# Gating and rounding of the output weights' pieces: kept in their traced place, one microsecond of plan time later

## The chip, the cores and the metric

The kernel runs on one core of a Trainium2 chip. The metric is the device time of one execution in microseconds (us). A core has a matrix engine (TensorE; PE in the rows, its weight loads PEld), VectorE (DVE), ScalarE (ACT), GpSimd (POOL) and SyncE (SP), whose queue issues nearly all DMAs here. Each of these takes its instructions strictly in the order in which they were laid down, so an instruction that waits holds up all that stands behind it on the same engine.

## The reference, cut to what matters

One layer of a diffusion trunk over 2048 latent tokens of width 1024, with 256 context tokens ahead of it. The part that the change touches is the output projection of the first half of the layer, whose columns are scaled by a gate:

```python
o, _, _ = token_mixers(h @ w_in[l], lb_f, lb_b, first, hf_c, hb_c, *mix_args)
x = x + g1 * (o @ w_out[l])
```

`g1` is one row of 1024 numbers that comes from the conditioning vector. `token_mixers` is a gated linear recurrence (four heads, two directions) and a spatial gating unit, both fed by the one big projection `h @ w_in`.

## The kernel before, in words

The tokens are taken in two halves of 1024. For each half the kernel runs a row of "banks": one bank is 128 output columns of `h @ w_in` for 512 tokens, eight k-steps of three matmuls each (each operand is split into a rounded high part and a rest, and high x high, low x high, high x low are summed: `xh`, `xl` for the tokens, `whi`, `wlo` for the weights). A weight block of 128 columns serves two banks. It is loaded as `raw` (L213, 512 KB), cast to `whi` on ACT (L131) and subtracted to `wlo` on DVE (L132). Between the k-steps the kernel calls two pumps. One, `hg_q`, feeds the work of the recurrence heads (matmuls on `Q` and `K` into `sc`, then on ACT, DVE and POOL the level updates: L500, L507, L578, L580, L802). The other, `bg_q`, feeds background work: the gate rows (`ada_block`), then the output weights (`w_out_ops`), the convolution taps and the down weights. A generator in a pump runs up to its next `yield w` and is resumed when the planned TensorE time has gone on by `w` us.

`w_out_ops` goes over 16 pieces of 128 x 512. A piece takes one of the three `raw` buffers, which it shares with the weight blocks of L213. One half of the buffer gets the weights (L945), the other the gate row spread over 128 partitions (L946). Later DVE multiplies them (L949), ACT rounds the product into `wo_hi` (L131, in a single buffer that is free again when the store of the piece before has landed), DVE subtracts for the low part (L132), and SP stores both to `wo_d` in DRAM (L951, L952), from where the output projection reads them much later (from 903 us on).

What is traced is then laid down by a scheduler, which may let an instruction pass others of its engine where it expects that they wait. `pin` (`keep_in_program_order`) forbids that for one instruction: it keeps its place in the traced order. In `split` the argument `keep` is applied to the ACT copy alone.

```python
def split(hi, lo, raw, eng=None, keep=lambda i: i):
    keep(S.copy(hi, raw))
    (eng or G).tensor_sub(lo, raw, hi.bitcast(F32))
```

When the last bank of half 0 is traced, the tokens of half 1 are loaded into `xh` and `xl` (L1069, L1070: 16 loads of 512 KB, each as soon as TensorE has used the old rows of its k-steps), and the banks of half 1 follow.

Of the kernel before, what the change touches and what calls it, by code (L numbers as in the profile page):

```python
# [10 lines left out]
F32R = mybir.dt.float32r  # L11
# [72 lines left out]
def tile_trunk(ctx, tc, x, c, cx, c_ctx, w_ada, b_ada, norm_mix, norm_ffn, w_in, hg_norm, sgu_g, sgu_b,  # L84
               w_sp, b_sp, w_out, w_up, conv_w, conv_b, w_down, norm_final, masks, out):
    nc = tc.nc
    V, S, G, T = nc.vector, nc.scalar, nc.gpsimd, Tensor(nc.tensor)
    ld = nc.sync.dma_start
    st = nc.sync.dma_start
    pin = tc.keep_in_program_order  # L90
# [38 lines left out]
# [4 lines that stand above are left out]
# [56 lines left out]
    with es1:  # L189
# [16 lines left out]
        def raw_tile():  # L206
            return p1.tile([P, D], F32, tag="raw", name="raw", bufs=3)
# [730 lines left out]
        def w_out_ops():  # L938

            for k in range(NK):  # L940
                for n in range(2):
                    cl = slice(n * 512, n * 512 + 512)
                    raw = raw_tile()
                    w, g = raw[:, :512], raw[:, 512:]
                    ld(w, w_out[k * P:(k + 1) * P, cl])  # L945
                    ld(g, g_d[0:1, cl].broadcast_to([P, 512]))  # L946
                    yield 5.0
                    hi = pm.tile([P, 512], F32, tag="acc", name="wo_hi")
                    V.tensor_mul(w, w, g)  # L949
                    split(hi.bitcast(F32R), g.bitcast(F32R), w, V)  # L950
                    st(wo_d[:, k, 0, cl], hi)  # L951
                    st(wo_d[:, k, 1, cl], g)  # L952
                    yield 2.5

        def w_down_ops():

# [19 lines left out]
        def head(hh, h):  # L976
# [18 lines left out]
            def pre_g():  # L995
                if prev[0] >= 0:
                    need(hg_q, (prev[0], prev[1], "keys"))
                else:
                    need(bg_q, "x1")
                    for e in range(8):  # L1000
                        bg_q.add(ada_block(e))
                    bg_q.add(w_out_ops())
                    bg_q.add(conv_taps())
                    bg_q.add(w_down_ops())
                t["F"] = pk.tile([P, 2, TH], F32, tag="F", name="F", align_bytes=AL)
                t["K"] = pk.tile([P, 2, TH], F32, tag="K", name="K", bufs=2, align_bytes=AL)
# [508 lines left out]
    for n, (u, i) in enumerate(prods):  # L1515
# [7 lines left out]
        hi, lo = u.A[i]  # L1523
# [37 lines left out]
    V = Kept(nc.vector, pin)  # L1561
# [243 lines left out]
```

## Time and profile before

| | us |
|---|---|
| three runs | 2458.63, 2462.23, 2462.24 |
| their median | 2462.23 |
| the profiled execution, own time | 2459.64 |
| its span in the trace | 2457.9 |
| TensorE busy | 2417.9 |
| VectorE busy | 1790.2 |
| ScalarE busy | 970.5 |
| GpSimd busy | 882.5 |

The span is the time from the first to the last instruction that the trace records. 1.7 us of the execution's own time lie outside it. Matmuls are pipelined, so that their recorded durations overlap (0.39 us each, 0.227 us from start to start).

### The profile page before, as it was taken

How to read it: one execution, taken by the hardware profiler on the slowest of the kernel's cores; microseconds unless marked ns; L12 is line 12 of the kernel's file. 1: busy time of each engine (PE TensorE's matmuls, PEld its weight loads, DVE VectorE, ACT ScalarE, POOL GpSimd, SP SyncE). 2: the span in 40 equal slices, each digit the busy share in tenths (PEclk: the TensorE clock that was granted, in tenths of full speed). 3: DMA queues.
4: the chain of work that ended last, by engine and by line, in shares of the span. 5: the costliest groups of instructions: out<-in, count | busy, mean ns of one | idle time of the engine just before them, and what ended most of it. 6: DMA issues, size and time to landing. Idle time of an engine off the chain costs nothing.

```text
span 2457.9 us, 32777 instructions
## 1 busy us (share of the span) xinstructions
PE 2417.9 (98%) x11859; PEld 2008.3 (82%) x11859; DVE 1790.2 (73%) x2445; ACT 970.5 (39%) x1614; POOL 882.5 (36%) x795
## 2 busy tenths in 40 slices
PE   7999999999999999999999999999999999999998
PEld 4888888888888888788788888888888888888887
DVE  5867785845766766465698878759999992776875
ACT  4554344434344442354443333333333342332343
POOL 1232110110121122100688787787777870000002
PEclk9999999999999999999999999999999999999999
DMA  8365446664354333768922222462222239844745
GB/s 308 109 208 164 146 129 202 198 214 146 103 180 155 99 103 104 260 205 269 300 90 85 91 80 90 163 250 93 84 89 94 87 102 348 312 127 147 227 150 197
DMA packets 307854, 400.12 MB, mean 163 GB/s; under 512 B 33113, under 2 KB 216161, under 8 KB 304621
## 3 DMA queue, kind: packets, MB, share of 16 engines
q1 hardware_dynamic: 304404, 397.28, 48.7%
q8 instruction: 94, 1.54, 0.3%
q10 hardware_dynamic: 3289, 0.76, 0.1%
q14 instruction: 67, 0.55, 0.1%
HBM read 288.85 MB, written 109.13 MB: 162 GB/s over the span
## 4 chain that ended last, share of the span: by engine, by line
PE 45%; DVE 7%; issue 3%; POOL 2%; ACT 2%; DMA 1%; SPq 0%; POOLq 0%; ACTq 0%; DVEq 0%
PE up L65 24%; PE dn L65 20%; DVE dn L1372 3%; DVE edges L1377 1%; DVE gp L1453 1%; ACT dn L1369 1%; POOL Al L132 1%; PE up L69 0%; PE pj L65 0%; POOL ra L1664 0%; DMA raw<-oT 0%; DMA xn<-cv 0%; POOL rr L1665 0%; DMA raw<-in_w_up_dram 0%; DVE keep L1447 0%
## 5 line engine op out<-in xcount | busy, mean ns | idle before, releaser
L1372 DVE SCALAR_TENSOR_TENSOR dn<-gp,taps,dn 128x1024 f32<-128x1024 f32 x352 | 448.2, 1279 | 21.3 <-ACT dn L1369 18.1
L65 PE MATMUL up<-yf,Ah 128*128 128x512 f32 x1232 | 393.6, 389 | 0.0
L65 PE MATMUL dn<-thl,mhl 128*128 128x512 f32 x1680 | 381.5, 389 | 1.2 <-ACT thl L131 1.2
L132 POOL TENSOR_TENSOR Al<-raw,Ah 128x512 fp32r<-128x512 f32 x264 | 343.3, 1309 | 87.8 <-ACT Ah L131 79.7
L65 PEld LDWEIGHTS dn<-thl,mhl 128*128 128x128 f32 x1680 | 315.1, 188 | 67.6 <-ACT thl L131 2.0
L65 PE MATMUL pj<-xh,whi 128*128 128x512 f32 x896 | 363.7, 406 | 0.0
L65 PE MATMUL pj<-xh,wlo 128*128 128x512 f32 x896 | 350.5, 391 | 3.0 <-DVE wlo L132 3.0
L65 PE MATMUL pj<-xl,whi 128*128 128x512 f32 x896 | 351.2, 392 | 1.0 <-POOL xl L132 1.0
L65 PE MATMUL up<-xah,Al 128*128 128x512 f32 x704 | 275.4, 391 | 2.9 <-POOL Al L132 2.8
L65 PE MATMUL up<-xah,Ah 128*128 128x512 f32 x704 | 274.5, 390 | 0.6 <-ACT Ah L131 0.6
L131 ACT CAST Ah<-raw 128x512 fp32r<-128x512 f32 x264 | 160.6, 618 | 278.5 <-PE up L65 212.3
L65 PEld LDWEIGHTS up<-yf,Ah 128*128 128x128 f32 x1232 | 231.2, 188 | 47.9
L65 PE MATMUL up<-xal,Ah 128*128 128x512 f32 x528 | 205.4, 389 | 0.0
L65 PE MATMUL up<-yf,Al 128*128 128x512 f32 x528 | 205.2, 389 | 0.0
L65 PEld LDWEIGHTS pj<-xh,wlo 128*128 128x128 f32 x896 | 168.3, 188 | 39.4 <-DVE wlo L132 3.7
L65 PEld LDWEIGHTS pj<-xh,whi 128*128 128x128 f32 x896 | 168.7, 188 | 33.2 <-issue 3.5
L65 PEld LDWEIGHTS pj<-xl,whi 128*128 128x128 f32 x896 | 168.9, 189 | 31.6 <-POOL xl L132 1.9
L65 PE MATMUL dn<-wo,o 128*128 128x512 f32 x768 | 182.9, 394 | 1.7 <-ACT o L131 1.1
L65 PEld LDWEIGHTS dn<-wo,o 128*128 128x128 f32 x768 | 141.9, 188 | 31.4 <-ACT o L131 1.6
L578 POOL TENSOR_TENSOR K<-K,tot 128x512 f32<-128x512 f32 x40 | 57.4, 1434 | 306.4 <-ACT K L580 222.4
L65 PEld LDWEIGHTS up<-xah,Al 128*128 128x128 f32 x704 | 132.1, 188 | 35.5 <-POOL Al L132 8.3
L132 DVE TENSOR_TENSOR wlo<-raw,whi 128x1024 fp32r<-128x1024 f32 x68 | 83.8, 1232 | 99.7 <-ACT whi L131 93.4
(315 smaller groups left out, 4021.6 us busy)
## 6 DMA issues: line engine op xcount, KB each, us to landing
raw<-in_w_up_dram SPq DMA_DIRECT2D x88, 512.0 KB, 4.6
mr<-m SPq DMA_DIRECT2D x85, 512.0 KB, 5.3
raw<-in_w_in_dram SPq DMA_DIRECT2D x68, 512.0 KB, 4.4
sT<-wd SPq DMA_DIRECT2D x88, 256.0 KB, 4.0
raw<-in_w_ada_dram SPq DMA_DIRECT2D x32, 512.0 KB, 4.0
yf<-yd SPq DMA_DIRECT2D x14, 1024.0 KB
m<-cv SPq DMA_DIRECT2D x22, 544.0 KB, 2.7
raw<-in_w_down_dram SPq DMA_DIRECT2D x22, 512.0 KB, 4.5
```

The lines of the kernel that those rows point to most:

```text
L65: return self.engine.matmul(out, lhsT, rhs, **kw)
L131: keep(S.copy(hi, raw))
L132: (eng or G).tensor_sub(lo, raw, hi.bitcast(F32))
L578: e.tensor_mul(view(K2, a * (2 * B + W), [[4 * B, n], [W + B - 2 * a * W, 2], [1, B]]), view(K, a * 2 * B, src), t)
L1369: S.activation(cr, gt[:, 0:RH, 0:GW], AF.Identity, bias=cvb[:, f:f + 1], scale=taps[:, f:f + 1])
L1372: V.scalar_tensor_tensor(out=cr, in0=gt[:, t // 3:t // 3 + RH, t % 3:t % 3 + GW], scalar=taps[:, t * NF + f:t * NF + f + 1], in1=cr, op0=A ...
L1377: V.scalar_tensor_tensor(out=e[:, 0, :], in0=gt[:, 1, t % 3:t % 3 + GW], scalar=taps[:, t * NF + f:t * NF + f + 1], in1=e[:, 0, :], op0=AL ...
L1453: V.tensor_add(g_rows(hh, f + c, n2), quad(p, kind), quad(add, kind))
```

## The change

The wait between the request for a piece and its gating grows from 5 to 6 us of planned TensorE time, and the wait to the next piece shrinks by as much. The product (L949) and the rounding copy (L131 into `wo_hi`) are pinned. The subtraction and the stores aren't.

```diff
                     ld(w, w_out[k * P:(k + 1) * P, cl])
                     ld(g, g_d[0:1, cl].broadcast_to([P, 512]))
-                    yield 5.0
+                    yield 6.0
                     hi = pm.tile([P, 512], F32, tag="acc", name="wo_hi")
-                    V.tensor_mul(w, w, g)
-                    split(hi.bitcast(F32R), g.bitcast(F32R), w, V)
+                    pin(V.tensor_mul(w, w, g))
+                    split(hi.bitcast(F32R), g.bitcast(F32R), w, V, pin)
                     st(wo_d[:, k, 0, cl], hi)
                     st(wo_d[:, k, 1, cl], g)
-                    yield 2.5
+                    yield 1.5
```

No instruction is added or taken away; their order changes. Three places follow.

VectorE at the end of head 2's gate banks of half 0. `wlo_3621` is the low part of the next weight block; `raw_3695` and `raw_3574` are pieces of the output weights. Before:

```order
L949 TENSOR_TENSOR raw_3634<-raw_3634 128x512
L132 TENSOR_TENSOR raw_3634<-raw_3634,wo_hi_3677 128x512
L949 TENSOR_TENSOR raw_3695<-raw_3695 128x512
L132 TENSOR_TENSOR wlo_3621<-raw_3618,whi_3620 128x1024
L779 TENSOR_TENSOR Q_3668<-qs_3174,F_3442 128x1024
```

And of the change:

```order
L949 TENSOR_TENSOR raw_3574<-raw_3574 128x512
L132 TENSOR_TENSOR raw_3574<-raw_3574,wo_hi_3607 128x512
L132 TENSOR_TENSOR wlo_3621<-raw_3618,whi_3620 128x1024
L779 TENSOR_TENSOR Q_3668<-qs_3174,F_3442 128x1024
L949 TENSOR_TENSOR raw_3631<-raw_3631 128x512
```

The fifth piece's product stood ahead of `wlo_3621`; now the third piece's work stands there, and the fourth product comes behind it.

SyncE where the tokens of half 1 are loaded. Before, the two weight blocks `raw_4529` and `raw_4617` are requested ahead of all 16 token loads, and no piece is among them:

```order
L213 DMA raw_4529<-in_w_in_dram 128x8x128
L674 DMA oT0_77<-nt_4257 128x512
L213 DMA raw_4617<-in_w_in_dram 128x8x128
L484 DMA tr_4650<-in_conv_w_dram 99x128
L1070 DMA xl_357<-xl_d_80 128x2x512
L1069 DMA xh_358<-xh_d_79 128x2x512 x2
L1070 DMA xl_357<-xl_d_80 128x2x512
```

The change, from the 14th piece's stores on; ten token loads stand behind the 15th's:

```order
L951 DMA wo_d_81<-wo_hi_4437 128x512
L952 DMA wo_d_81<-raw_4403 128x512
L1070 DMA xl_357<-xl_d_80 128x2x512
L1069 DMA xh_358<-xh_d_79 128x2x512
L945 DMA raw_4508<-in_w_out_dram 128x512
L946 DMA raw_4508<-g_d_76 128x512
L1070 DMA xl_357<-xl_d_80 128x2x512
L951 DMA wo_d_81<-wo_hi_4491 128x512
L952 DMA wo_d_81<-raw_4452 128x512
L1069 DMA xh_358<-xh_d_79 128x2x512
```

Its end, where `raw_4529` and `raw_4617` are requested behind the last token load:

```order
L1069 DMA xh_358<-xh_d_79 128x2x512
L1070 DMA xl_357<-xl_d_80 128x2x512
L213 DMA raw_4529<-in_w_in_dram 128x8x128
L951 DMA wo_d_81<-wo_hi_4572 128x512
L952 DMA wo_d_81<-raw_4508 128x512
L213 DMA raw_4617<-in_w_in_dram 128x8x128
```

The pieces and the two weight blocks have changed places around the token loads.

ScalarE at the start of half 1. `sig_4565` and `sig_4614` belong to the first two banks of half 1 (`pj_4535` and `pj_4574`, which the change calls `pj_4568`); `whi_4531` is the weight block of the third. Before:

```order
L131 CAST whi_4531<-raw_4529 128x1024
L553 ACTIVATE F_4362<-pj_4475 128x512
L558 ACTIVATE K_4363<-pj_4475 128x256x2
L972 ACTIVATE sig_4565<-pj_4535 128x512
L787 COPY sc_4584<-sc_4585 128x512
L787 COPY sc_4584<-sc_4591 128x512
L131 CAST whi_4619<-raw_4617 128x1024
L972 ACTIVATE sig_4614<-pj_4574 128x512
```

And of the change:

```order
L787 COPY sc_4584<-sc_4585 128x512
L972 ACTIVATE sig_4565<-pj_4535 128x512
L787 COPY sc_4584<-sc_4591 128x512
L131 CAST wo_hi_4572<-raw_4508 128x512
L972 ACTIVATE sig_4614<-pj_4568 128x512
L131 CAST whi_4531<-raw_4529 128x1024
L131 CAST whi_4619<-raw_4617 128x1024
```

The cast of the third bank's weights moved from ahead of the first bank's sigmoid to behind the second's. On VectorE its subtraction (`wlo_4532`) stands likewise behind the product with that sigmoid (`sgt`, L973).

## Rows read from the trace of the kernel before

**Rows 1.** The page's busy times: engine, busy us, share, instructions.

```profile
PE 2417.9 (98%) x11859; PEld 2008.3 (82%) x11859; DVE 1790.2 (73%) x2445; ACT 970.5 (39%) x1614; POOL 882.5 (36%) x795
```

**Rows 2.** Windows: stretch, length, busy us by engine, TensorE clock, DMA share, GB/s.

```profile
395.00:410.00 15.00, 15.00 (x70) 12.32 (x68) 2.63 (x4) 6.46 (x10) 0.00 (x0) 1.00 0.57 196
410.00:425.00 15.00, 12.89 (x65) 10.76 (x65) 11.30 (x13) 6.29 (x10) 0.00 (x0) 1.00 0.53 175
440.00:530.00 90.00, 89.99 (x499) 77.48 (x499) 50.60 (x86) 36.47 (x55) 10.60 (x10) 1.00 0.76 255
```

**Rows 3.** Waits of TensorE, 365 to 600 us: in total, times, longest.

```profile
PE pj L65 <- DVE wlo L132: 2.1, 1, 2.1
PE sc L65 <- ACT K L580: 1.2, 2, 0.8
```

**Rows 4.** Timeline of TensorE: start, length, what, idle before it.

```profile
409.84 0.39 PE L65 MATMUL pj<-xl,whi 128*128 128x512 f32 x1
412.34 0.50 PE L65 MATMUL pj<-xh,wlo 128*128 128x512 f32 x1 [2.11 <-DVE wlo L132]
```

**Rows 5.** Timeline of VectorE there.

```profile
410.46 0.69 DVE L949 TENSOR_TENSOR raw<-raw 128x512 f32<-128x512 f32 x1 [10.54 <-DMA raw<-g_d]
411.07 1.22 DVE L132 TENSOR_TENSOR wlo<-raw,whi 128x1024 fp32r<-128x1024 f32 x1
```

**Rows 6.** Timeline of ScalarE there.

```profile
404.14 1.05 ACT L131 CAST whi<-raw 128x1024 fp32r<-128x1024 f32 x1 [2.77 <-PE pj L65]
```

**Rows 7.** Timeline of SyncE's queue there.

```profile
401.30 0.57 SPq L952 DMA_DIRECT2D wo_d<-raw  x1
406.86 0.33 SPq L945 DMA_DIRECT2D raw<-in_w_out_dram  x1
407.25 0.42 SPq L946 DMA_DIRECT2D raw<-g_d  x1
```

**Rows 8.** Rounding casts of all pieces by tile: duration ns, first and last start.

```profile
L131 ACT CAST wo_hi<-raw x16: 610/621/624, 382.0 to 495.3; 128x512 fp32r<-128x512 f32 x16
```

**Rows 9.** Timeline of TensorE at two level matmuls.

```profile
433.42 2.19 PE L65 MATMUL sc<-Q,K 128*128 128x128 f32 x16 [0.40 <-ACT K L580]
539.45 2.19 PE L65 MATMUL sc<-Q,K 128*128 128x128 f32 x16 [0.81 <-ACT K L580]
```

**Rows 10.** Timeline of SyncE's queue around the token loads of half 1.

```profile
499.40 0.38 SPq L213 DMA_DIRECT2D raw<-in_w_in_dram  x1
...
505.47 0.38 SPq L1070 DMA_DIRECT2D xl<-xl_d  x1
...
518.81 0.55 SPq L1070 DMA_DIRECT2D xl<-xl_d  x1
```

**Rows 11.** Windows, the token loads under way.

```profile
515.00:520.00 5.00, 5.00 (x24) 4.14 (x23) 1.68 (x2) 2.54 (x3) 0.00 (x0) 1.00 1.05 408
```

**Rows 12.** Timeline of TensorE, the first two banks of half 1.

```profile
517.48 0.39 PE L65 MATMUL pj<-xh,whi 128*128 128x512 f32 x1
...
522.70 0.39 PE L65 MATMUL pj<-xh,wlo 128*128 128x512 f32 x1
...
524.97 1.95 PE L65 MATMUL sc<-qs,kd 128*128 128x128 f32 x16
...
530.90 2.82 PE L65 MATMUL sc<-Q,K 128*128 128x128 f32 x16
...
533.59 0.48 PE L65 MATMUL pj<-xh,whi 128*128 128x512 f32 x1
```

**Rows 13.** Timeline of ScalarE, start of half 1.

```profile
523.12 0.60 ACT L972 ACTIVATE sig<-pj 128x512 f32<-128x512 f32 x1 [3.10 <-PE pj L65]
...
530.88 1.04 ACT L131 CAST whi<-raw 128x1024 fp32r<-128x1024 f32 x1 [3.33 <-PE pj L65]
```

**Rows 14.** Timeline of VectorE, start of half 1.

```profile
513.10 1.23 DVE L132 TENSOR_TENSOR wlo<-raw,whi 128x1024 fp32r<-128x1024 f32 x1 [14.25 <-ACT whi L131]
514.24 1.22 DVE L779 TENSOR_TENSOR Q<-qs,F 128x1024 f32<-128x1024 f32 x1
...
531.95 1.23 DVE L132 TENSOR_TENSOR wlo<-raw,whi 128x1024 fp32r<-128x1024 f32 x1 [7.51 <-ACT whi L131]
```

**Rows 15.** Landing of the low parts' stores (L952), all 16.

```profile
DMA to landing us min/median/max: 2.0/2.2/2.4
```

## Prediction

> **What bounds the kernel now.** I read the page first: TensorE is busy for 2417.9 of 2457.9 us [rows 1]. A change that adds no instruction can therefore only act through TensorE's waits. The pieces' casts run from 382.0 to 495.3 [rows 8], so I asked for TensorE's waits in the stretch around them and some way behind. There are three, in two rows [rows 3]: once 2.1 us for the low weights `wlo`, twice a level matmul for a copy of `K`, 1.2 us together. The windows agree: 12.89 busy us of 15 in the one stretch with the long wait, and 89.99 of 90 from 440 to 530 [rows 2]. The timeline then shows the chain of the long wait backward. The matmul with `wlo` starts at 412.34 [rows 4], as `wlo` ends on DVE at 412.29. That subtraction started at 411.07, though its input `whi` had been cast by 405.19 [rows 6]. It stood behind the fifth piece's product, for which DVE idled 10.54 us until the gate row landed at 410.46 [rows 5]. The gate row was requested at 407.25, because its buffer came free only when a store issued at 401.30 had landed; SP took the next request at 406.86 [rows 7]. Normally such a store lands in 2.2 us [rows 15]; here it was 5.5.
>
> **The change part by part.**
>
> *The pins and the microsecond.* The 16 products, 16 casts, 16 subtractions and 64 DMAs stay as they are, so their own work is worth nothing either way. What counts is what stands behind them.
>
> *The long wait.* In the new order `wlo_3621` stands ahead of the fourth product and behind the third piece's. I stepped that piece through: its request now goes out at about 385, so its data are there by 391; its cast stands on ACT behind the copies of the second gate bank's end (near 398.6 by counting matmuls back from 409.84), so its subtraction is over by 401.6. DVE is then free when `whi` is ready at 405.2, `wlo` ends at 406.4, and TensorE wants it at 410.07. The wait goes with 3.6 us to spare. It is worth 412.34 - 409.84 - 0.227 = 2.27 us from start to start (the row's 2.11 counts from the modelled end). Term: -2.3, bounds -2.3 and 0 (if DVE were blocked 3.6 us longer after all).
>
> *The level matmul at 433.42.* TensorE arrives 2.27 us sooner, but the chain of DVE, ACT and POOL that makes `K` only about 1.9 sooner: the fifth piece's cast now stands behind both copies of `sc`, so that DVE waits for it before the next `wlo`. The wait of 0.40 [rows 9] becomes about 0.8. Term: +0.4, bounds 0 and +1. From there to 500 us I found no product whose data come later than DVE gets to it.
>
> *The token loads of half 1.* Before, SP issues them from 505.47 to 518.81, with no piece between [rows 10]. Now the 14th's stores, the 16th's requests and the 15th's stores stand among them. The 15th's product comes on DVE behind the `wlo` that starts at 513.10, its cast (0.62 us [rows 8]) follows at 515.0, and its subtraction stands behind `Q` (1.22 us [rows 14]), so it ends near 516.9. Less the 2.2 us that TensorE is ahead, the store goes out at about 514.7 and the first of the last ten loads at 515.1. The loads run at 408 GB/s while they are under way [rows 11], so 524 kB take 1.29 us; a store (0.65) and ten loads from 515.5 end near 529.1, landed by 529.6 to 530.1. When are they wanted? The first bank of half 1 starts at 517.48 [rows 12], 515.3 in the change. Ahead of the matmul with the last load stand 43 projection matmuls (9.7 us at 0.227 from start to start, 517.48 to 522.70 being 23 of them), eight `sc` of 1.70 (524.97 to 526.67), eight of 2.66 (530.90 to 533.59, less a transpose) and two transposes (0.26): 529.7. So it lands as it is wanted; I take 0 to 0.3 and book it under the next term, with 1.7 as upper bound.
>
> A page of the Trainium skill speaks against this: "DMA: Bandwidth & Descriptors", section "Where 436 GB/s comes from", has a transfer from HBM to SBUF bound by about 358 GB/s rather than by the fabric. By that figure ten loads take 14.6 us instead of 12.9, and the sum below would come out 1.7 us higher. The row's 408 GB/s decides here.
>
> *The third bank's weights.* Before, `raw_4529` is requested at 499.40 [rows 10] and its cast stands ahead of the first bank's sigmoid. Now the request follows the last token load, and the cast follows the sigmoid of the second bank, which can't start before that bank ends. With t the start of the bank's last matmul: the sigmoid starts at t + 0.42 (522.70 to 523.12 [rows 12, 13]) and takes 0.60, the cast 1.04 [rows 13], so TensorE gets `whi` at t + 2.1 instead of t + 0.23. It has four matmuls (0.9 us) that need `whi` alone. `wlo` takes 1.23 from t + 2.1 [rows 14], so the fifth starts at t + 3.37 instead of t + 1.13. Term: +2.24, whatever the DMAs do; there was no wait here before. The load itself, behind ten others, lands at 531 to 532, and t + 1.0 is 531.6. So +0.3 more (0 to 2). Sum: +2.5.
>
> *The level matmul at 539.45.* It waited 0.81 for `K` [rows 9], 0.98 from start to start. The new wait ahead of it gives the chain time, while `whi_4619`, whose load is late as well, stands ahead of the copies on ACT. I count about 0.6 left. Term: -0.4, bounds -1 and +1.
>
> *The end.* The order is the same from there on. TensorE's idle of 2.11 us left its granted clock at 1.00 in that window [rows 2], so I book no term for the clock.
>
> Sum: -2.3 + 0.4 + 2.5 - 0.4 = +0.2. A stall of 2 us at 412 goes, and one of the same size comes at about 533.
>
> **The rivals.**
>
> *A, the forecast:* the stall moves to the third bank of half 1 and the time stays, span 2458.1. For it: ACT's order puts the cast behind a sigmoid that needs the bank's end. Against it: three waits must come out as stepped.
>
> *B, nothing comes in its place.* The cast is early enough for a reason that I overlook. Then 2.3 and the 0.98 are gained, 3.2 us (0.13%): span 2454.7. For it: from 440 to 530 TensorE lost 0.01 us with eight pieces under way [rows 2]. Against it: the order on ACT.
>
> *C, slower: the token loads come late.* SP waits at the stores of the 14th and 15th pieces with loads behind them, and each us by which the last load lands after 529.7 goes straight to TensorE. It decides from about 5 us. The store that took 5.5 instead of 2.2 us to land [rows 7, 15] shows how a store fares behind 512 KB loads. SP has one such wait for a landing (16th request behind the 14th's store), and about 2 us of slack in front of the 15th's store, so one late landing costs 1.2, two such delays or a 15th store held by 5 us cost 5 to 9: 2465 to 2470. For it: before, these loads had only a little to spare (the last issued at 518.81 [rows 10], wanted near 529.7). Against it: the stores' place follows from DVE and ACT, which have little else there.
>
> *D, a gain over 0.2%.* All three waits together are 3.3 us, and 0.2% is 4.9. It would need a wait outside the stretch to go.
>
> *E, the change does little:* only 32 of the 48 instructions of engines are pinned, and the scheduler lays subtractions and stores anew. If the new places meet as many late gate rows as the old, the time is also that of before; it falls together with A in the time, and the long wait at 412 would tell it apart.
>
> **How the numbers follow.** The profiled execution took 2459.64, and the median of the three runs is 2462.23, 2.6 higher: the runs differ by 3.6 among themselves with no change at all. The mean of those four times is 2460.7, and with +0.2 to 0.3 I predict 2461.0. About 0.2% (4.9 us) is what a measurement of this kernel can tell from no change. Chances: A and E 0.58, B 0.25, C 0.13, D 0.04. A and B both fall within 0.2%, but for a little at the edge on either side. So faster 0.05, same 0.82, slower 0.13. The range: B against the mean of the four gives 2457.4 and a fast run of it about a us less, hence 2456.5; A with its upper bounds (+1, +1.7, +2, and 2462.2 as base) reaches 2467, and the lower end of C 2465, hence 2466.5. What is left out is most of C and the tail of B.
>
> **What would show it.** In the changed profile: no wait of TensorE for `wlo` at 410, and `wlo_3621` on DVE by 407. A wait of about 0.8 at the second level of head 2. At 531 to 535, two short waits of TensorE, first for `whi` (L131 on ACT, near 1.8) and then for `wlo` (near 0.4), with SP's last token load issued near 520 instead of 518.81. The fourth term is right if the level matmul behind it waits less than 0.81. Rows of TensorE that wait for `xh` or `xl` DMAs would speak for C. The prediction is wrong if the third bank of half 1 starts without a wait (B), if the token loads hold TensorE for more than 2 us (C), or if DVE still waits for a gate row with a `wlo` behind it.

## The result, and the profile after

| | before | changed |
|---|---|---|
| median of 20 runs | 2462.14 us | 2465.59 us |
| lowest and highest | 2458.63, 2464.19 | 2463.29, 2468.50 |
| the profiled execution, own time | 2459.64 | 2466.21 |
| its span | 2457.9 | 2464.4 |

The ratio is 1.0018, with a 95% interval of 1.0012 to 1.0024: slower by 3.0 to 5.9 us. That is just under the 0.2% that the prediction called no change, and inside its range, but it is a loss, and the forecast was +0.2 us. The predicted value of 2461.0 is 4.6 too low. 1.4 of that is the base: the prediction started from 2460.7, and the median of 20 runs before is 2462.14.

TensorE's waits around the pieces come first, as in [rows 3]. The columns are what waited for what, the total, the number and the longest.

```profile
PE pj L65 <- DMA xl<-xl_d: 2.3, 3, 0.8
PE pj L65 <- ACT whi L131: 1.6, 1, 1.6
PE pj L65 <- DMA xh<-xh_d: 0.9, 1, 0.9
PE sc L65 <- ACT K L580: 0.4, 1, 0.4
```

The wait for `wlo` is gone. So is one of the two for `K`. The other three rows are new, and all of them lie at the start of half 1. The timeline of TensorE says where:

```profile
429.90 1.35 PE L65 MATMUL sc<-Q,K 128*128 128x128 f32 x9 [0.43 <-ACT K L580]
...
517.66 0.50 PE L65 MATMUL pj<-xl,whi 128*128 128x512 f32 x1 [0.74 <-DMA xl<-xl_d]
...
520.22 0.50 PE L65 MATMUL pj<-xh,whi 128*128 128x512 f32 x1 [0.91 <-DMA xh<-xh_d]
...
530.50 0.50 PE L65 MATMUL pj<-xl,whi 128*128 128x512 f32 x1 [0.75 <-DMA xl<-xl_d]
...
533.09 0.50 PE L65 MATMUL pj<-xl,whi 128*128 128x512 f32 x1 [0.80 <-DMA xl<-xl_d]
...
536.14 0.79 PE L65 MATMUL pj<-xh,whi 128*128 128x512 f32 x1 [1.62 <-ACT whi L131]
```

Four matmuls wait for a token load, two in the first bank of half 1 and two in the second. One, the first of the third bank, waits for `whi`. The gain is where the prediction put it. The windows (columns as in [rows 2]) show TensorE busy without a gap around 412, where it was busy for 12.89 of 15 us before:

```profile
395.00:410.00 15.00, 15.00 (x68) 12.42 (x67) 5.43 (x7) 6.86 (x11) 0.00 (x0) 1.00 0.59 193
410.00:425.00 15.00, 15.00 (x80) 13.10 (x79) 9.41 (x12) 6.38 (x9) 0.00 (x0) 1.00 0.57 168
```

VectorE's timeline there answers [rows 5]: `wlo` starts at 404.08, and the fourth product stands behind it and behind `Q`.

```profile
404.08 1.23 DVE L132 TENSOR_TENSOR wlo<-raw,whi 128x1024 fp32r<-128x1024 f32 x1 [3.54 <-ACT whi L131]
...
406.36 0.69 DVE L949 TENSOR_TENSOR raw<-raw 128x512 f32<-128x512 f32 x1
```

Now SyncE's queue at the token loads, which answers [rows 10]. The "..." leave out loads, a store, the gate row of a request and one weight request.

```profile
498.87 0.37 SPq L1070 DMA_DIRECT2D xl<-xl_d  x1
...
500.99 1.51 SPq L1069 DMA_DIRECT2D xh<-xh_d  x2
505.18 0.34 SPq L951 DMA_DIRECT2D wo_d<-wo_hi  x1
...
506.83 0.75 SPq L1069 DMA_DIRECT2D xh<-xh_d  x1
510.55 0.35 SPq L945 DMA_DIRECT2D raw<-in_w_out_dram  x1
...
511.42 0.42 SPq L1070 DMA_DIRECT2D xl<-xl_d  x1
511.97 0.38 SPq L951 DMA_DIRECT2D wo_d<-wo_hi  x1
513.01 0.32 SPq L952 DMA_DIRECT2D wo_d<-raw  x1
513.38 0.48 SPq L1069 DMA_DIRECT2D xh<-xh_d  x1
513.92 1.06 SPq L1070 DMA_DIRECT2D xl<-xl_d  x1
...
521.47 1.35 SPq L1070 DMA_DIRECT2D xl<-xl_d  x1
522.87 1.17 SPq L213 DMA_DIRECT2D raw<-in_w_in_dram  x1
```

Before, the first eight loads went out in one run from 505.47 to 509.07. Now SyncE stands three times with loads behind it: from 502.5 to 505.18 at the 14th piece's store, from 507.6 to 510.55 at the 16th piece's request, and at the two stores of the 15th. SyncE's waits from 500 to 525 name what the first two of these are for:

```profile
SPq L945 <- DMA wo_d<-raw: 2.9, 1, 2.9
SPq L951 <- ACT wo_hi L131: 2.6, 1, 2.6
```

The eighth load goes out at 513.92, 4.9 us later than before, while TensorE is ahead: the first bank of half 1 starts at 513.80, 3.7 us earlier than the 517.48 of [rows 12].

What SyncE stands for from 502.5 on is the 14th piece's rounded product. VectorE has the product at 498.06, but on ScalarE the pinned cast stands behind the `F` and `K` of a gate bank that TensorE has yet to finish. VectorE's line first, then ScalarE's:

```profile
497.37 0.69 DVE L949 TENSOR_TENSOR raw<-raw 128x512 f32<-128x512 f32 x1
```

```profile
503.12 0.60 ACT L553 ACTIVATE F<-pj 128x512 f32<-128x512 f32 x1 [3.49 <-PE pj L65]
503.62 1.11 ACT L558 ACTIVATE K<-pj 128x512 f32<-128x512 f32 x1
504.50 0.65 ACT L131 CAST wo_hi<-raw 128x512 fp32r<-128x512 f32 x1
```

The `K` before was through at 499.63, and SyncE saw the 13th piece's last store landed at 500.54, so the cast could have begun near 500.5; it began at 504.50. The 16th piece's request then waits for the landing of this piece's low part, which is issued at 505.91 and landed at 510.53, after 4.6 us. (The 2.0 to 2.4 of [rows 15] are not of all 16 stores: the trace shows the landing of only two of them directly.)

What this does to the transfers is in the last two columns of the windows, the DMA engines' share and GB/s:

```profile
510.00:512.00 2.00, 2.00 (x11) 1.65 (x10) 2.00 (x3) 1.52 (x2) 0.00 (x0) 1.00 0.93 353
512.00:514.00 2.00, 2.00 (x10) 1.69 (x9) 0.98 (x2) 0.00 (x0) 0.00 (x0) 1.00 0.71 187
514.00:516.00 2.00, 2.00 (x10) 1.65 (x9) 1.37 (x2) 1.63 (x2) 0.00 (x0) 1.00 0.67 194
516.00:518.00 2.00, 1.26 (x7) 0.71 (x6) 2.00 (x2) 0.00 (x0) 0.00 (x0) 1.00 1.04 401
518.00:530.00 12.00, 10.74 (x58) 8.81 (x56) 5.20 (x7) 2.28 (x4) 0.00 (x0) 1.00 1.05 406
```

From 512 to 516 the DMA engines move about half of what they move before and behind. SyncE had issued nothing from 507.6 to 510.55, and what it issued then, the weights of the 16th piece, took 4.2 us to land. At 408 GB/s [rows 11] those 4 us would have carried 0.87 MB more, some 2.1 us of transfer. That the standstill emptied the engines is read from this order in time; the run with closer pieces below bears on it. Then they run full until the last load is in.

The third bank's weights, on ScalarE:

```profile
534.55 0.60 ACT L972 ACTIVATE sig<-pj 128x512 f32<-128x512 f32 x1 [8.68 <-PE pj L65]
535.05 1.04 ACT L131 CAST whi<-raw 128x1024 fp32r<-128x1024 f32 x1
```

The cast stands behind the second bank's sigmoid and starts as soon as that is through, as predicted. Its data were there already.

The last thing was not in any rival. Behind the waits TensorE's clock falls (the column ahead of the DMA share, a mean over the stretch), and its matmuls come 0.43 us apart instead of 0.227:

```profile
535.00:540.00 5.00, 3.86 (x9) 3.09 (x10) 3.41 (x4) 3.27 (x4) 0.00 (x0) 0.54 0.65 196
540.00:545.00 5.00, 5.00 (x18) 3.95 (x18) 3.21 (x4) 1.20 (x1) 0.00 (x0) 0.78 0.62 195
```

From 536.14 to 542.25, 14 steps take 6.11 us instead of 3.18: 2.9 us. It is the lower of the two levels, 1.2 instead of 2.4 GHz, after four waits of 0.7 to 0.9 us and one of 1.6 within 19 us.

**Where the time went.** The transposes of `K` (L69) come once in each head and are the same in all kernels here, so their starts cut every execution into the same pieces of work. In us, with the experiments that follow below:

| kernel | 2nd to 3rd `K` (holds 412) | 3rd to 4th (holds the token loads) | 4th to 7th | 7th to 8th |
|---|---|---|---|---|
| before | 96.35 | 98.91 | 279.01 | 94.37 |
| the change | 93.81 | 107.48 | 279.13 | 94.35 |
| the change, 2nd and 3rd trace | 93.84, 93.78 | 104.65, 106.26 | 279.09, 278.82 | 94.42, 94.38 |
| waits alone (e1yield) | 95.35 | 98.90 | 279.00 | 94.41 |
| pins alone (e2pins) | 93.79 | 104.88 | 279.07 | 94.37 |
| held 30 us (e3late) | 93.80 | 99.66 | 279.38 | 93.88 |
| held 15 us (e4wlate) | 93.79 | 100.20 | 279.65 | 93.90 |
| closer pieces (e5short) | 93.78 | 103.37 | 278.62 | 94.39 |
| held 6 us (e6one) | 93.87 | 103.52 | 278.48 | 93.94 |
| held 55 us (e7hold) | 93.84 | 98.70 | 278.83 | 96.81 |
| six pieces pinned (e8early) | 94.29 | 100.48 | 279.58 | 94.38 |
| held 40 us (e10forty) | 93.79 | 98.68 | 278.73 | 93.53 |

The change gains 2.54 us in the first stretch and loses 8.57 in the second, 2.9 of it to the clock. The three starts are 375.10, 468.91 and 576.39 in the change, and 376.24, 472.59 and 571.50 before. The 1.1 us by which the change is ahead at the first of them are there at the first `K` already (276.05 against 277.13), 100 us ahead of the pieces' casts, and are none of its doing.

### The profile page after: what moved, and what is told of

Same layout as the page of the kernel before. It is cut to its first block, busy times and chain, and to the rows that moved or that the text cites. A ratio compares the mean times of both kernels' runs of the same rounds, so it can differ in the third digit from the quotient of the medians.

```text
span 2464.4 us, 32770 instructions
## 1 busy us (share of the span) xinstructions
PE 2419.7 (98%) x11859; PEld 2008.9 (82%) x11859; DVE 1790.1 (73%) x2445; ACT 969.6 (39%) x1614; POOL 878.6 (36%) x795
## 5 line engine op out<-in xcount | busy, mean ns | idle before, releaser
L131 ACT CAST Ah<-raw 128x512 fp32r<-128x512 f32 x264 | 160.6, 618 | 279.1 <-PE up L65 217.7
L65 PEld LDWEIGHTS up<-xah,Ah 128*128 128x128 f32 x704 | 132.2, 188 | 28.2 <-ACT Ah L131 1.4
```

The source lines that it names most:

```text
L65: return self.engine.matmul(out, lhsT, rhs, **kw)
```

## The experiments

**Which half of the change does it?** First the two waits alone, without the pins:

```diff
-                    pin(V.tensor_mul(w, w, g))
-                    split(hi.bitcast(F32R), g.bitcast(F32R), w, V, pin)
+                    V.tensor_mul(w, w, g)
+                    split(hi.bitcast(F32R), g.bitcast(F32R), w, V)
```

> The waits of 6.0 and 1.5 us alone, without the pins. Theory (the pins move the pieces into the half switch, the microsecond does nothing by itself): the order of SyncE's queue at the half switch is that of before, so the time is before's within 1.5 us, the wait of 2.1 us for wlo near 412 is still there, no wait of TensorE for xl or xh, clock 1.00 from 510 to 560. Rival (the microsecond shifts the pieces into the half switch): about +3.5 us, token-load waits as in the change.

Measured: ratio to before 0.9998 (0.9989 to 1.0007), median 2460.32 against 2461.16. No wait for a token load, and the wait for `wlo` is still there, though 1.2 instead of 2.1 us in this execution:

```profile
PE pj L65 <- DVE wlo L132: 1.2, 1, 1.2
```

Then the pins alone, with the old waits:

```diff
-                    yield 6.0
+                    yield 5.0
...
-                    yield 1.5
+                    yield 2.5
```

> The two pins alone, with the old waits of 5.0 and 2.5 us. Theory (the pins do it all): the time of the change, +3.0 to +4.5 us against before; four waits of TensorE for xl or xh of 0.7 to 0.9 each, one of about 1.6 for whi, the granted clock below 1.00 between 535 and 545. Rival (the microsecond matters): the time of before within 1.5 us, or the wait near 412 comes back, +5 us or more.

Measured: 1.0015 (1.0006 to 1.0024), 2465.09 against 2461.16. The same four waits for token loads (2.3 in three and 0.9) and the 1.62 for `whi`, and none for `wlo`. The pins are the change; the microsecond does nothing that could be measured. Which of the two pins does it, the product's or the cast's, no run here tells apart. One part of the expectation missed: the clock stayed at 1.00 from 530 to 546, and still the second stretch is 5.97 longer than before. So the fall of the clock is not needed for the loss.

**Is the whole loss at the token loads?** The change, with the last three pieces held until the loads are issued:

```diff
-                    yield 1.5
+                    yield 1.5 if (k, n) != (6, 0) else 30.0
```

> The change, with the 14th to 16th piece held back until the token loads of half 1 are issued. Theory (the whole loss lies at the half switch: about 4.5 us of token loads, 1.8 of the third bank's weights, 2.9 of a lower clock behind them): no wait for xl, xh or whi between 510 and 540, clock 1.00 there, the level wait of 0.8 at 539 back, the 2.1 at 412 still gone, so before less 2.3: 2459 to 2460.5. Rival (the pins cost elsewhere, or the three pieces stall as much behind the loads): 2462 or more.

Measured: 0.9992 (0.9984 to 1.0001), median 2459.23 against 2461.16. No wait for `xl`, `xh` or `whi`, clock 1.00, nothing at 412. The theory holds, though the time is 1.9 and not 2.3 below before, and the level wait came out at 1.50 instead of 0.8:

```profile
536.89 2.19 PE L65 MATMUL sc<-Q,K 128*128 128x128 f32 x16 [1.50 <-ACT K L580]
```

The same with 15 us, which leaves the third bank's cast behind the second sigmoid (`else 15.0`):

> As the one before, but held for 15 us instead of 30: the token loads are free of pieces, while the third bank's weights are still cast behind the second bank's sigmoid. Theory (the clock falls behind the row of token-load waits, and the weights cost their own 1.8 to 2.3): a wait of 1.6 to 2 us for whi, none for xl or xh, clock 1.00, the level wait behind it gone: before -2.3 +2.0 -1.0, about 2460.8. Rival (the wait for whi alone lowers the clock): another 2.9 us, about 2463.7, with matmuls 0.43 us from start to start behind it.

Measured: 0.9999 (0.9991 to 1.0008), 2460.59 against 2461.16, as the theory's sum has it, but not by its way: there was no wait for `whi`. In this order ten level matmuls stood between the second bank and the third (528.16 to 529.95) and covered the late cast. Two waits behind it, 0.63 and 0.62, stand there instead, and the stretch is 1.29 longer than before. So this run does not price the late weights; it shows that they cost little where other work stands between two banks (0.28 more than usual ahead of the first matmul with `wlo`, 530.75 to 531.26).

**How much among the loads does it take?** Pieces closer together, so that behind the first load two pairs of stores and a weight block stand among the loads, and no request:

```diff
-                    yield 1.5
+                    yield 0.8
```

> The change with 0.8 instead of 1.5 us between pieces: the 14th... pieces run ahead, so that behind the first token load only two pairs of stores and one weight block stand among the loads, and no request of a piece (0.5 MB less, and no wait of SyncE for a landing). Theory (the loads are late by what the queue moves and waits for ahead of them): the waits for xl and xh shrink from 3.2 us in four to 2 or less, the wait for whi stays near 1.6, and the clock falls less or not: 1 to 2.5 us over before. Rival (the lateness comes from SyncE standing at the first pair of stores alone): the same four waits as in the change, +3.5 us.

Measured: 1.0013 (1.0004 to 1.0022), 2464.58 against 2460.32. That is +3.2 in the middle of the interval, where 1 to 2.5 had been expected; the first two stretches of this one trace add up to +1.9. The waits from 365 to 600 are as expected: 1.0 for the loads instead of 3.2, and the clock at 1.00.

```profile
PE pj L65 <- ACT whi L131: 1.6, 1, 1.6
PE pj L65 <- DMA xl<-xl_d: 1.0, 2, 0.7
```

The rival is out: SyncE stands at the 14th piece's store for as long as in the change (from 502.86 to 505.79, the cast being just as late), and still two of the four waits are gone. SyncE's queue there, and a window behind it, in which the DMA engines don't run empty:

```profile
505.79 0.33 SPq L951 DMA_DIRECT2D wo_d<-wo_hi  x1
```

```profile
506.00:516.00 10.00, 10.00 (x45) 8.26 (x44) 4.81 (x6) 4.57 (x6) 0.00 (x0) 1.00 1.06 405
```

What is missing against the change is the 16th piece's request: its 0.5 MB, and the 2.9 us that SyncE waits at it.

The three pieces held 6 us longer (`else 6.0`): one request and one pair of stores among the loads, 1 MB.

> The change, the 14th to 16th piece held 6 us longer: 1 MB of pieces (one request and one pair of stores) stands behind the first token load, all other loads follow in a row, and the third bank's weights are requested behind the last load. Theory (a token load has about 5 us to spare, so 2.6 us of traffic costs nothing; the whole loss needs the 2 MB and the waits of the change): no wait for xl or xh, at most the late weights, clock 1.00: within 1.5 us of before, below it rather. Rival (any piece among the token loads costs): waits for xl or xh of 1 us or more.

Measured: 1.0008 (0.9999 to 1.0018), 2463.22 against 2460.32. No wait for a load, so 1 MB among them is carried by their spare time. But the second stretch is 4.6 us longer than before. The late weights show at full price here, in a wait for `whi` alone, with the clock at 1.00, and two waits further on follow:

```profile
533.80 0.50 PE L65 MATMUL pj<-xh,whi 128*128 128x512 f32 x1 [1.62 <-ACT whi L131]
542.07 0.66 PE L69 MATMUL mi<-ident,vv 128*128 128x128 f32 x4 [0.82 <-ACT vv L587]
544.07 1.11 PE L65 MATMUL sc<-Q,K 128*128 128x128 f32 x7 [0.78 <-ACT K L580]
```

The expectation of no more than 1.5 us over before lies inside the interval (-0.2 to +4.4), but the median is 2.9 over, and "below it rather" was wrong in the trace: 93.87 and 103.52 are 2.1 more than before. SyncE stands at the 14th's store here too (505.10 to 507.01).

**Towards a version that keeps the gain.** The three pieces held for 55 us (`else 55.0`):

> The change, the 14th to 16th piece held for 55 us, so that they come behind the levels of the head as well. Theory (in the run held for 30 us the three pieces' casts and products made the level wait 1.5 instead of 0.8): level wait 0.8, otherwise as with 30 us: 2.3 to 3 us below before. Rival (the level wait of 1.5 has another reason): 1.5 remains, no better than 30 us.

Measured: 1.0006 (0.9997 to 1.0015), 2462.32 against 2460.32. The level wait was 0.84, as expected, and the second stretch 98.70, better than before. But a wait came up where nobody had looked, some 380 us later, in another head:

```profile
917.86 2.05 PE L65 MATMUL sc<-Q,K 128*128 128x128 f32 x16 [2.90 <-ACT K L580]
```

What put it there isn't settled.

The pins on the first six pieces only:

```diff
-                    hi = pm.tile([P, 512], F32, tag="acc", name="wo_hi")
-                    pin(V.tensor_mul(w, w, g))
-                    split(hi.bitcast(F32R), g.bitcast(F32R), w, V, pin)
+                    hi = pm.tile([P, 512], F32, tag="acc", name="wo_hi"); keep = pin if k < 3 else (lambda i: i)
+                    keep(V.tensor_mul(w, w, g))
+                    split(hi.bitcast(F32R), g.bitcast(F32R), w, V, keep)
```

> The change with the pins on the first six pieces only; the other ten are free to pass others. Theory (the pins of the first pieces remove the wait near 412, those of the last ones move them among the token loads): no wait for wlo at 412, no piece among the token loads and none of the waits behind them: before less 2.3, some 2459. Rival (the free pieces meet other late gate rows in head 2's stretch): a wait for wlo or K of 1 us or more between 410 and 500, and the time of before.

Measured: 1.0002 (0.9993 to 1.0011), 2461.16 against 2460.32. No wait for `wlo`, no piece among the loads, no wait for them: those parts held. But a new wait at 477.68 takes 1.07 back (with 0.16 more from start to start), and the forecast of 2459 did not come. That is the rival's case, for another tile than it named:

```profile
477.68 3.84 PE L65 MATMUL mi<-vt,kt 128*128 128x128 f32 x32 [1.07 <-DVE nt L697]
```

**Does the clock fall every time?** The changed kernel itself, twice more.

> The changed kernel itself, for another trace. Theory (the lower clock behind the waits is a matter of the single execution; the pins alone had the same waits without it): the four waits for xl and xh and the one for whi again, 5.5 to 6 us more than before from 472 to 571 if the clock stays at 1.00, some 8.5 if it falls; the rest as in the first trace. Rival (the clock falls in every execution of the change): matmuls 0.43 us from start to start behind the wait for whi, 8.5 us more in that stretch.

> The changed kernel once more, for how often the clock falls behind the waits; expected as for the second trace.

Measured: single executions of 2464.40 and 2467.07. Both have the four waits and the 1.62 for `whi`. The clock stayed at 1.00 in the second trace and fell in the third, to 0.82 here and to 0.84 in the next 5 us:

```profile
535.00:540.00 5.00, 3.32 (x10) 2.20 (x10) 2.76 (x3) 3.46 (x4) 0.00 (x0) 0.82 0.75 190
```

So it is a matter of the single execution: 2.9, 0 and about 1.6 us (106.26 less 104.65) in three traces of one kernel. The second trace, at full clock, is the one from which the waits themselves can be priced:

```profile
517.02 0.39 PE L65 MATMUL pj<-xh,whi 128*128 128x512 f32 x1
518.27 0.50 PE L65 MATMUL pj<-xl,whi 128*128 128x512 f32 x1 [0.86 <-DMA xl<-xl_d]
518.60 0.39 PE L65 MATMUL pj<-xh,wlo 128*128 128x512 f32 x1
...
534.27 0.40 PE L65 MATMUL pj<-xh,wlo 128*128 128x512 f32 x1
536.28 0.50 PE L65 MATMUL pj<-xh,whi 128*128 128x512 f32 x1 [1.62 <-ACT whi L131]
```

From start to start, less the usual 0.227, the four load waits take 1.02, 1.09, 0.80 and 1.13, and the matmul behind each starts 0.1 late as well: 4.45 together. The third bank takes 1.78 at `whi`, 0.23 at `wlo` (537.08 to 537.54) and 0.11 behind each: 2.23. The level matmul behind them no longer waits: -0.98. The sum is 5.70, and the stretch is 104.65 - 98.91 = 5.74 longer.

**Held for 40 us** (`else 40.0`): behind the first four levels of the head, ahead of its end.

> The change with the 14th to 16th piece held for 40 us: behind the first four levels of the head, but ahead of its end. Theory (what the pins gain near 412 is kept if the held pieces disturb neither the token loads nor the levels): 2.5 us less up to 472, no more than 0.5 lost from there to 571, nothing behind it: 2 to 3 us under before. Rival (the pieces cost as much wherever they come): a new wait of 1 us or more between 530 and 620 or near 910, and the time of before.

Measured: 0.9986 (0.9977 to 0.9995), median 2456.01 against 2460.03. That is faster than before by 1.2 to 5.7 us, and so faster than the change too. The 2 to 3 us that were expected lie inside; the trace has 2.8 of it up to the fourth `K`, and 0.8 more from the seventh to the eighth, which nobody had foreseen. Only the level waits are left of all those from 365 to 600:

```profile
PE sc L65 <- ACT K L580: 1.2, 2, 0.8
```

## Why the prediction was wrong

**The long wait (-2.3) and the level at 433 (+0.4): right place, better than forecast.** `wlo` stands where it was expected and starts at 404.08 ("on DVE by 407"). The level wait stayed at 0.43 instead of growing to 0.8. Together the stretch gained 2.54 where 1.9 was booked. Without the pins (e1yield) the wait for `wlo` is still there.

**The third bank's weights (+2.24): right.** 2.23 at full clock, with the two waits that were named (1.62, "near 1.8", and a short one for `wlo`). That the sum agrees to 0.01 is luck in part: from start to start the one for `wlo` is 0.23 instead of about 0.4, and 0.22 for the late matmuls behind the two had not been booked. The 0.3 more for a late load did not come.

**The level at 539 (-0.4): right in sign**, 0.98 gained, since the waits ahead gave the chain more time than was counted.

**The token loads (0 to 0.3, at most 1.7): the step that failed.** They cost 4.45. The prediction reckoned "a store (0.65) and ten loads from 515.5 end near 529.1", and asked for the last load alone. Three things were wrong in it.

- It started the reckoning at the 15th's store and took the six loads ahead of it as done. In fact SyncE had stood at the 16th's request for 2.9 us. The sixth load went out at 511.42 and the seventh at 513.38, and the first bank wants them at the k-steps that then wait: 2.3 of the 4.45 lie there (1.02, 1.09 and 0.1 behind each), at 517.66 and 520.22 in the first trace, where the prediction expected nothing. The place of the 15th's store itself was right: 0.6 us ahead of the first bank was forecast, and 0.8 came (513.01 against 513.80).
- It took the DMA engines as always full. They ran at 187 to 194 GB/s from 512 to 516, behind the 2.9 us in which SyncE issued nothing.
- It took the ten loads and a store, 5.5 MB, as all that was carried. From 515.5 to 533.1 the engines carried 7.0 MB in the trace, at 398 GB/s. The third bank's weights, issued at 522.87 behind the last load, were carried alongside the loads, not behind them: from 530 to 533.1 the trace has nearly a thousand packets of 512 bytes, as only the weight blocks have them, among those of 2 KB. The last load itself went out at 521.47 and not "near 520", since SyncE held several loads until earlier transfers had landed (2.0 us in all), and was in use 11.6 us later (533.09).

This is rival C, which had 0.13, and its mechanism in the main ("SP waits at the stores of the 14th and 15th pieces with loads behind them"). It was priced at 1.2 for one late landing and 5 to 9 for more, for the last load alone, and put aside with the words that the stores' place follows from engines that "have little else there". That was an error behind the error: what had gone unlooked at was what stands ahead of a pinned cast. The 14th piece's cast waited on ScalarE for the `F` and `K` of a bank that wasn't computed yet (503.12 to 504.50 above), and with it its store, the loads behind the store, and the 16th's request.

The runs bear out that the pieces among the loads are the cause: with none there (15, 30, 40 and 55 us, and the six pinned pieces) no matmul waits for a load. They also show that the late cast alone is not enough. With closer pieces and with 6 us more it is as late, and the waits for loads are 1.0 and none. What only the change and the pins alone have is the request of the 16th piece behind the late store, at which SyncE waits 2.9 us for a landing. How much of the 4.45 is that standing and how much the extra bytes, no run here takes apart.

The page that was weighed against the forecast, the Trainium skill's "DMA: Bandwidth & Descriptors", section "Where 436 GB/s comes from", would have cost 1.7 us here by its 358 GB/s. The loads were late, but not by that rule: once fed, the DMA engines carried 401 to 406 GB/s from 516 to 530. The same page of the Trainium skill says in "Issuing engines are not separate DMA queues" that DMAs interleave on the same 16 engines whichever engine issued them. No run here tests that, since SyncE issues nearly all of them; what the trace shows is that DMAs of this one issuer interleave (the packets from 530 to 533.1 above).

**The clock: no term was booked**, by [rows 2], where one wait of 2.11 left it at 1.00. Five waits within 19 us did not always leave it there. It is 0 to 2.9 us of an execution, and it widens the distance between the two profiled executions (6.6 us) beyond that of the medians (3.45).

The sum by measured terms is -2.54 + 4.45 + 2.23 - 0.98 = +3.2, without the clock; the medians say +3.45, and the ratio 3.0 to 5.9. With 1.5 for the clock, the mean of three traces, it would be +4.7, inside the interval as well, so how often the clock falls in the 20 runs stays open. So does the rest of the kernel: from the eighth `K` to the end of the span the traces of the change take 1514.6 to 1515.9 against 1513.0 before, and other kernels spread over 1513.3 to 1516.3 there.

## What to carry to other kernels

A queue that issues strictly in order charges each wait to all that stands behind it: where stores or requests come to stand among loads, step through the queue's own times from the first load on, not from the last store, and ask of every load when it is wanted, not of the last alone. Pinning an instruction to its traced place orders it there, but also holds it behind whatever its engine still waits for, and an in-order issuer passes that delay on to transfers that have nothing to do with it. The 40 us run kept the gain of the pins and moved three pieces past the token loads; but with 15, 30 or 55 us the same edit gave less, so each place must be looked at by its own profile.

## What was not expected of the hardware

- TensorE's clock fell behind a row of short waits in two of three traces of one kernel, and not in the third: mean granted clock 0.54, 1.00 and 0.82 from 535 to 540, with the same waits ahead (0.6 to 0.9 four times, then 1.62).
- A matmul that had waited was followed by the next after 0.33 to 0.34 us instead of 0.227 (518.27 to 518.60 above), so that each short wait cost 0.1 more than the step to the waiting matmul shows.
- With the queue full, a 512 KB load was in use 11.6 us after its issue (521.47 to 533.09), while the DMA engines moved 398 GB/s.
